# Input norm of a hybrid encoder layer: the row factor moved from the product's operand to its results

## The chip, the cores and the metric

The kernel runs on one core of a Trainium2 chip. The metric is the device time of one execution in microseconds (us), lower is better. The kernel before takes 3166.97 us, the median of three runs (3166.91 to 3171.95).

## The reference

One encoder layer on x of 2048 rows (tokens) by 1024 columns, all in f32:

```python
u = _rms_norm(h, norm_mix_g[l])          # h * rsqrt(mean(h*h) + 1e-6) * g, row by row
proj = u @ w_in[l]                       # 1024 x (1536 + 1024 + 512 + 512 + 16)
hy = _short_conv_centred(proj[..., :HY_COLS], hy_conv_w[l], hy_conv_b[l])      # three taps along the rows
spec = _hyena_filter_spectrum(L, ...)    # a small network with two sines over 2048 positions gives the filters
y_hy = _group_rms_norm(_hyena(hy, spec, hy_skip[l]), hy_norm_g[l], HYENA_GROUPS)   # long convolutions
qk = jax.nn.silu(_short_conv_centred(proj[..., HY_COLS:off], ml_conv_w[l], ml_conv_b[l]))
y_ml = ...                               # bidirectional mLSTM, then a group norm
h = h + concat(y_hy, y_ml) @ w_out[l]
```

Cross attention, a squared-ReLU MLP and a final norm follow. The change touches the first two lines alone: the row factor rsqrt(mean(h*h) + 1e-6) of `u` belongs to a token, the weight g to one of the 1024 columns over which the product sums. So the factor may be multiplied in before the product or after it; g only before.

## The kernel before, in words

**Products.** Each product of f32 operands is made of three: both operands are split into a high half, rounded to the matmul's type by ScalarE (`copy`, shown as CAST), and a low half, the rest, made by VectorE (`split`, L344 and L345). `mm3` (L339 to L342) issues hi by hi, hi by lo and lo by hi into one PSUM bank of 128 by 512.

**The first product, computed transposed.** Columns of `proj` stand on partitions, tokens along the free axis. `sweep` (from L656) takes 256 columns of w_in at a time (`c2`); for each of them two chunks of 512 tokens (`c`) and two halves of 128 columns (`m`); a group is 8 steps of the inner dimension times 3 matmuls, 24 in all. ScalarE copies the full bank to a tile P (L690). When both chunks of a P are there, the short convolution is done in three operations (ScalarE L704, VectorE L706 and L707), and put on `pending`; the next group's end runs `sweep_out`: eight transposes on TensorE (L724), copies, stores to DRAM. Tokens come in two halves of 1024: first `sweep(range(4), 0, True)` on tokens 0 to 1023, then `sweep(range(4), 1, False)` on the others, four 256-column pieces each; the other columns follow later, again by halves.

**The first half's operand.** `x_first` (L489 to L574) prepares tokens 0 to 1023, in chunk 0 (tokens 0 to 511) and chunk 1. x arrives transposed, in loads of two pieces of 128 by 512 each. For chunk 0 ScalarE squares the pieces (L535), VectorE adds them (L537), TensorE sums over partitions (L540), `inv_rms` (L415) makes the factor by Newton steps on a 128 by 4 tile, `diagonal` (L448) and `spread` (L454) turn it into a row on all partitions by a product with ones (L457) and a ScalarE copy (L461). `gained` (L465) multiplies each piece by weight and factor in one VectorE operation; ScalarE makes the high half (L500), VectorE the low half (L502). For chunk 1 the factors come from 2 MB of x in natural layout, whose row sums ScalarE makes as it squares (L422). A function `rest`, run within the first group, writes chunk 1's pieces and starts the stream of weights.

**Work beside it.** `filters` (L234 to L325) runs woven into the sweeps: for four chunks of 512 positions a load of features (L265, issued by SP), a product (L267), a sine (six VectorE operations, L248 to L257, and ScalarE's Sin, L258), a second product (L271) and a second sine; then 32 filter pairs: two products at a time (L177 and L188), VectorE (L317, L318, L322), GpSimd (L323), a transform (`front`, again L177 and L188), ScalarE copies (L301), and a store (L303). The filters and `hy` go through DRAM to the long convolutions (loads `a<-hy`, `a<-fs`; products L845), which are woven with the rest of the sweeps. `row_stats` (L430) makes the row sums of tokens 1024 to 2047, `x_chunk` (L479) their scaled and split pieces, both a step at a time from `pop` in the sweeps. `weights` (L358) loads and splits each next 256 columns in four pieces (L374).

**What sets the order.** The functions issue instructions in program order; a scheduler then places them by priorities along a simulated timeline, held in some places by `keep_in_program_order`. The result is one fixed list per engine, executed in order; each instruction waits for semaphores of those it needs. SP issues most DMAs, also in one fixed order. So a moved operation can shift what stands next to what on every engine.

Of the kernel before, what the change touches and what calls it, by code (L numbers as in the profile page):

```python
# [133 lines left out]
class Prog:  # L134
    def __init__(self, ctx, tc, a):
# [16 lines left out]
        self.banks = []  # L152
        self.pending = []
        self.prepq = None
        self.mid = None
# [333 lines left out]
    def x_first(self):  # L489
        nc, sb = self.nc, self.isb  # L490
        pin = self.tc.keep_in_program_order
        c0, c1 = slice(0, 512), slice(512, 1024)

        def write(xs, cs, rb, between=lambda k: None):
            for k in range(9):
                if k < 8:
                    d = self.gained(xs[k], self.g_mix[:, k:k + 1], rb)
                    if k:
                        pin(d)
                    pin(nc.scalar.copy(self.xh[:, k, cs], xs[k]))  # L500
                if k:
                    nc.vector.tensor_tensor(self.xl[:, k - 1, cs], xs[k - 1], self.xh[:, k - 1, cs].bitcast(F32), ALU.subtract)  # L502
                between(k)

        def pieces(ts):
            return [ts[k // 2][:, k % 2] for k in range(8)]

        x0 = []
# [4 lines left out]
        wsrc = self.items[0][0].rearrange("(k p) c -> p k c", p=128)  # L513
        w0 = [sb.tile([128, 8, 256], F32R, tag=tag, name=tag, bufs=2) for tag in ("wh", "wl")]
        raw = [self.ta().rearrange("p k c -> p (k c)").rearrange("p (k c) -> p k c", k=4) for i in range(2)]
        for i in range(2):
            nc.sync.dma_start(out=raw[i], in_=wsrc[:, 4 * i:4 * i + 4])
        nat = []
        for i in range(4):
            rows = self.a["x"][512 + 128 * i:640 + 128 * i]  # L520
            if i < 2:
                xn = sb.tile([128, D], F32, tag="xn", name="xn", bufs=2)
                nc.sync.dma_start(out=xn, in_=rows)
                nat += [xn[:, 0:512], xn[:, 512:1024]]
            else:
                for h in range(2):
                    xn = self.tb()
                    nc.sync.dma_start(out=xn, in_=rows[:, 512 * h:512 * h + 512])
                    nat.append(xn)
        x1 = pieces([self.x_load(1, j, self.ta()) for j in range(4)])  # L530

        ssum = sb.tile([128, 512], F32, tag="rb", name="ssum", bufs=2)
        for k in range(8):
            sq = sb.tile([128, 512], F32, tag="st", name="sq", bufs=3) if k else ssum
            pin(nc.scalar.activation(sq, x0[k], AF.Square))  # L535
            if k:
                nc.vector.tensor_tensor(ssum, ssum, sq, ALU.add)  # L537
        p = self.mm()
        for t in range(4):
            nc.tensor.matmul(p[:, t:t + 1], ssum[:, 128 * t:128 * t + 128], self.ones[:, 0:1], start=True, stop=True)  # L540
        self.inv_rms(self.rx[:, 0:4], p[:, 0:4])
        dg = self.diagonal(self.rx[:, 0:4])
        ss = sb.tile([128, 2, 4], F32, tag="ss", name="ss", bufs=2)

        def nat_sum(i):
            self.square_sum(nat[i], ss[:, i % 2, i // 2:i // 2 + 1])

        for k in range(0, 8, 2):
            ks = slice(k, k + 2)
            self.split(w0[0][:, ks], w0[1][:, ks], raw[k // 4][:, k % 4:k % 4 + 2])  # L550
        for i in range(4):
            nat_sum(i)
        self.wst = iter((w0,))
        rb = self.spread(dg)
        later = []

        def between(k):
            if k < 4:
                nat_sum(4 + k)
            if k == 4:  # L560
                self.close_sums(self.rx[:, 4:8], ss)
                later.append(self.diagonal(self.rx[:, 4:8]))
        write(x0, c0, rb, between)

        def rest():
            write(x1, c1, self.spread(later[0], True))
            w1 = self.weights(sb, *self.items[1], kc=2, nbufs=3, pin=True)
            self.wst = self.stream(sb, self.items[2:], w1, kc=2, nbufs=3)
        self.mid = rest
        for _ in range(9):  # L570
            yield
        for c in (2, 3):
            yield from self.row_stats(self.rx[:, 4 * c:4 * c + 4], self.a["x"][512 * c:512 * c + 512])
        yield from self.row_stats(self.rm, self.a["mem"])  # L574

    def pop(self, n=1):
        for _ in range(n):
            if self.prepq is not None and next(self.prepq, 0) == 0:
                self.prepq = None

    def prep_x(self, hf):
        self.prepq = chain(self.x_chunk(2 * hf), self.x_chunk(2 * hf + 1))
# [74 lines left out]
    def sweep(self, cols, hf, first, after=None):  # L657
        nc, a, sb = self.nc, self.a, self.isb
        xh, xl, cw, cb, carry = self.xh, self.xl, self.cw, self.cb, self.carry
        for c2 in cols:  # L660
            wh, wl = next(self.wst)
            Ps = []
            if hf == 0:
                off, use, t0, n = 1, 0, 0, 1008 if first else 1040
            elif first:
                off, use, t0, n = 0, 15, 1040, 1008
            else:
                off, use, t0, n = 17, 0, 1008, 1040
            for c in range(2):
                for m in range(2):  # L670
                    yield 5.5
                    cc = carry[:, 2 * c2 + m]
                    ms = slice(128 * m, 128 * m + 128)
                    cs = slice(512 * c, 512 * c + 512)
                    p = self.mm()
                    for k in range(8):
                        self.mm3(p, wh[:, k, ms], wl[:, k, ms], xh[:, k, cs], xl[:, k, cs], k == 0, k == 7)
                        if k == 5 and self.mid is not None:
                            f, self.mid = self.mid, None
                            f()  # L680
                    if c == 0:
                        P = sb.tile([128, 1088], F32, tag="P", name="P", bufs=2)
                        Ps.append(P)
                        edge = 0 if hf == 0 else 1024 if first else 1041
                        nc.vector.memset(P[:, edge:edge + 1], 0.0)  # L685
                        if not first:
                            e0 = 1025 if hf == 0 else 0
                            nc.vector.tensor_copy(P[:, e0:e0 + 17], cc)
                    P = Ps[m]
                    nc.scalar.copy(P[:, off + 512 * c:off + 512 * c + 512], p)  # L690
                    if c == 0:
                        if self.pending:
                            self.pending.pop(0)()
                        self.pop(2)
                        if m == 1 and c2 == cols[-1] and after is not None:
                            after()
                        continue
                    self.pop(3 - 2 * m)
                    if first:
                        nc.vector.tensor_copy(cc, P[:, 1008:1025] if hf == 0 else P[:, 0:17])  # L700
                    ct = 2 * c2 + m
                    cv = sb.tile([128, 1088], F32, tag="cv", name="cv", bufs=2)
                    v = cv[:, 0:n]
                    nc.scalar.activation(v, P[:, use + 1:use + 1 + n], AF.Identity, bias=cb[:, ct:ct + 1],  # L704
                                         scale=cw[:, 1, ct:ct + 1])
                    nc.vector.scalar_tensor_tensor(v, P[:, use:use + n], cw[:, 0, ct:ct + 1], v, ALU.mult, ALU.add)  # L706
                    nc.vector.scalar_tensor_tensor(v, P[:, use + 2:use + 2 + n], cw[:, 2, ct:ct + 1], v, ALU.mult, ALU.add)  # L707
                    if ct >= 12:
                        nc.scalar.activation(v, v, AF.Silu)
                        if ct >= 16:  # L710
                            nc.vector.tensor_scalar(v, v, 128.0 ** -0.5, None, ALU.mult)
                    self.pending.append(lambda ct=ct, cv=cv, t0=t0, n=n: self.sweep_out(ct, cv, t0, n))

    def sweep_out(self, ct, cv, t0, n):
        nc, sb = self.nc, self.isb
        v = cv[:, 0:n]
# [1224 lines left out]
def program(p):  # L1941
    with ExitStack() as ms:
        with ExitStack() as es:
# [79 lines left out]
```

## Time and profile before

| | |
|---|---|
| median of three runs | 3166.97 us |
| the profiled execution | 3178.03 us, span 3176.3 us |
| mean granted TensorE clock | 0.982 |
| HBM | 191 GB/s over the span |
| costliest group on VectorE | L345, low halves of weights, 289.5 us busy |

How to read it: the span runs from the first to the last instruction of one profiled execution. Busy time of an engine is what its instructions took; matmuls are pipelined, so the busy times of neighbouring ones overlap, and what one costs is the distance to the start of the next. In the lists of groups a row has line, engine, operation, result and operands, count, busy time, mean of one, and the idle time before them with what ended it. In the timeline a row begins with start and busy time in us, and ends with the idle time before it and what released it, in brackets. The granted clock is a share of TensorE's full speed. PEld is TensorE loading weights.

### The profile page before, as it was taken

Reading aid. Unit: us, or ns where it says so; the run is one execution under the profiler, and the core shown is the slowest. Engines: PE = TensorE matmul, PEld = TensorE weight load, DVE = VectorE, ACT = ScalarE, POOL = GpSimd, SP = SyncE. Lnnn points to the kernel's source line nnn. Section 1 sums busy time; section 2 is a strip of 40 time slices with the busy share of each in tenths; the row PEclk is TensorE's granted clock in tenths of the full one; section 3 lists DMA queues with packets and bytes.
Section 4 is the critical chain, followed back from the end, with each engine's and each line's share of the span. In section 5 each row is a group of like instructions: output and inputs, shape, how many; then the busy total and the mean of one; then the engine's idle time right before and its main releaser. Section 6 shows DMA issues by size and latency. Waiting matters only on the chain.

```text
span 3176.3 us, 43590 instructions
## 1 busy us (share of the span) xinstructions
PE 3039.3 (96%) x14473; PEld 2393.8 (75%) x14473; DVE 2048.0 (64%) x3563; ACT 1503.0 (47%) x2873; POOL 1157.8 (36%) x802
## 2 busy tenths in 40 slices
PE   6999999999999976999999999999999999999998
PEld 4655566776668766788888888888888878888876
DVE  7775466434865676878766566657655686565695
ACT  5543366523675343445454455556555443333335
POOL 0122012100112334324231426776555483434483
PEclk9999999999999998999999999999999999999999
DMA  5554767686576988547374747656644474444434
GB/s 190 191 196 162 255 194 205 180 253 212 165 226 191 309 256 263 172 144 231 114 272 144 274 131 246 203 194 221 216 155 146 163 243 147 144 129 152 123 93 169
DMA packets 447673, 609.48 MB, mean 192 GB/s; under 512 B 39118, under 2 KB 249166, under 8 KB 446424
## 3 DMA queue, kind: packets, MB, share of 16 engines
q1 hardware_dynamic: 409268, 548.18, 54.7%
q10 hardware_dynamic: 38180, 58.51, 5.5%
q8 instruction: 115, 1.88, 0.2%
q14 instruction: 110, 0.90, 0.1%
HBM read 404.15 MB, written 202.41 MB: 191 GB/s over the span
## 4 chain that ended last, share of the span: by engine, by line
PE 79%; DMA 8%; DVE 7%; issue 3%; ACT 2%; POOL 1%; SPq 0%; ACTq 0%; DVEq 0%; POOLq 0%
PE mm L340 17%; PE mm L342 17%; PE mm L341 17%; PE hy L342 5%; PE hy L340 5%; PE hy L341 5%; PE hy L177 3%; PE hy L876 2%; PE mm L845 2%; PE hy L918 1%; DMA xt<-in_x_t_dram 1%; DVE wl L345 1%; PE hy L1213 1%; PE hy L1082 1%; PE hy L1215 1%
## 5 line engine op out<-in xcount | busy, mean ns | idle before, releaser
L345 DVE TENSOR_TENSOR wl<-wn,wh 128x512 fp32r<-128x512 f32 (+1 forms) x364 | 289.5, 830 | 128.9 <-ACT wh L345 128.7
L1558 DVE TENSOR_TENSOR bl<-wr,bh 128x512 fp32r<-128x512 f32 x213 | 239.1, 1129 | 130.8 <-ACT bh L1557 130.6
L1557 ACT CAST ah<-w 128x512 fp32r<-128x512 f32 x284 | 176.7, 623 | 303.3 <-PE hy L341 156.1
L345 ACT CAST wh<-wn 128x512 fp32r<-128x512 f32 (+1 forms) x364 | 208.1, 619 | 218.7 <-PE mm L342 51.2
L923 POOL TENSOR_TENSOR b<-b,a 128x512 f32<-128x512 f32 x64 | 87.2, 1363 | 586.8 <-ACT b L921 463.2
L340 PE MATMUL mm<-xh,wh 128*128 128x512 f32 x640 | 271.6, 425 | 3.7 <-ACT xh L500 2.3
L341 PE MATMUL mm<-xl,wh 128*128 128x512 f32 x640 | 257.9, 404 | 2.4 <-DVE xl L345 1.8
L342 PE MATMUL mm<-xh,wl 128*128 128x512 f32 x640 | 259.2, 405 | 0.0
L1557 ACT CAST bh<-wr 128x512 fp32r<-128x512 f32 x232 | 143.7, 621 | 233.3 <-PE mm L342 181.1
L1558 DVE TENSOR_TENSOR al<-w,ah 128x512 fp32r<-128x512 f32 x236 | 214.4, 909 | 54.3 <-ACT ah L1557 52.9
L342 PE MATMUL mm<-bh,al 128*128 128x512 f32 x576 | 225.3, 394 | 7.3 <-DVE al L1558 4.7
L340 PE MATMUL mm<-bh,ah 128*128 128x512 f32 x576 | 226.9, 394 | 1.0 <-DVE acc L1715 0.9
L341 PE MATMUL mm<-bl,ah 128*128 128x512 f32 x576 | 226.1, 393 | 0.0
L340 PE MATMUL mm<-act,wh 128*128 128x512 f32 x512 | 198.4, 393 | 2.6 <-ACT wh L345 1.3
L341 PE MATMUL mm<-act,wh 128*128 128x512 f32 x512 | 200.4, 392 | 0.2 <-DVE act L345 0.2
L342 PE MATMUL mm<-act,wl 128*128 128x512 f32 x512 | 199.0, 391 | 0.0
L340 PE MATMUL hy<-bh,ah 128*128 128x512 f32 x448 | 175.2, 391 | 0.0
L341 PE MATMUL hy<-bl,ah 128*128 128x512 f32 x448 | 174.6, 390 | 0.0
L342 PE MATMUL hy<-bh,al 128*128 128x512 f32 x448 | 174.4, 390 | 0.0
L340 PEld LDWEIGHTS mm<-xh,wh 128*128 128x128 f32 x640 | 122.0, 191 | 65.7 <-issue 29.2
L341 PEld LDWEIGHTS mm<-xl,wh 128*128 128x128 f32 x640 | 121.6, 190 | 53.0 <-issue 24.4
L323 POOL TENSOR_TENSOR b<-b 128x512 f32<-128x512 f32 x32 | 59.1, 1848 | 275.8 <-DVE P L685 127.8
(378 smaller groups left out, 8487.2 us busy)
## 6 DMA issues: line engine op xcount, KB each, us to landing
wr<-hc SPq DMA_DIRECT2D x224, 256.0 KB
w<-in_ff_w_dram SPq DMA_DIRECT2D x172, 256.0 KB
hc<-wn SPq DMA_DIRECT2D x128, 256.0 KB
wn<-in_w_in_dram SPq DMA_DIRECT2D x100, 256.0 KB
hc<-q SPq DMA_DIRECT2D x96, 256.0 KB
fs<-a SPq DMA_DIRECT2D x32, 512.0 KB
a<-fs SPq DMA_DIRECT2D x64, 256.0 KB
a<-zs SPq DMA_DIRECT2D x64, 256.0 KB
```

What stands on the lines that cost most here:

```text
L177: b = self.nc.tensor.matmul(*products[-1], start=True, stop=True)
L323: nc.gpsimd.tensor_tensor(e[1], f, b, ALU.subtract)
L340: mm(ps, lh, rh, start=start, stop=False)
L341: mm(ps, lh, rl, start=False, stop=False)
L342: mm(ps, ll, rh, start=False, stop=stop)
L345: both = (self.nc.scalar.copy(hi, src), self.nc.vector.tensor_tensor(lo, src, hi.bitcast(F32), ALU.subtract))
L845: nc.tensor.matmul(pp, dm[:, m], t[:, m], start=True, stop=True)
L876: nc.tensor.matmul(pg, em[:, m], y, start=True, stop=True)
L918: nc.tensor.matmul(pp, dm[:, m], t[:, m], start=True, stop=True)
L923: nc.gpsimd.tensor_tensor(xt, xt, hi[:, m], ALU.mult)
L1557: self.nc.scalar.copy(hi, src)
L1558: eng.tensor_tensor(lo, src, hi.bitcast(F32), ALU.subtract)
```

## The change

The pieces of the first 1024 tokens are multiplied by g alone: ScalarE makes the high half from x as a copy scaled by g, VectorE the low half from x in one operation. Nothing of chunk 0's operand needs the row factor any more. The loads of x and of the first weights alternate; the 2 MB in natural layout are not loaded. Squares of chunk 0 come after its split; a function `second` run in group 0 makes chunk 1's operand, starts the weights and squares chunk 1; `scales`, run in group 1, makes column sums, factors and rows for both chunks into `rowb[0]` and `rowb[1]`. What was done as a bank is left is put into a closure `leave`, kept on a list `lag` for up to three groups (fewer towards the eighth), and in the first sweep over the first half VectorE multiplies the bank by `rowb[c]` as it writes P, in place of ScalarE's copy. Later sweeps copy as before. A pool `x_o` for the sums and rows is closed between the two sweeps by `opened`. Which pending store is run, and when `pop` is called, moves slightly.

```diff
+        for j in range(4):                      # x_first, loads
             x0.append(self.x_load(0, j, ...))
+            if j % 2 == 0:
+                nc.sync.dma_start(out=raw[j // 2], in_=wsrc[:, 2 * j:2 * j + 4])
...
+        def operand(xs, c, k):
+            to = (slice(None), k, slice(512 * c, 512 * c + 512))
+            g = self.g_mix[:, k:k + 1]
+            pin(nc.scalar.activation(self.xh[to], xs[k], AF.Copy, scale=g))
+            nc.vector.scalar_tensor_tensor(self.xl[to], xs[k], g, self.xh[to].bitcast(F32), ALU.mult, ALU.subtract)
...
+        def columns(c):
+            p = self.hy()
+            for t in range(4):
+                nc.tensor.matmul(p[:, t:t + 1], ssum[c][:, 128 * t:128 * t + 128], self.ones[:, 0:1], start=True, stop=True)
+            rx = self.rx[:, 4 * c:4 * c + 4]
+            self.inv_rms(rx, p[:, 0:4])
+            self.dg = self.diagonal(rx)
+
+        def rows(c):
+            p = self.hy()
+            nc.tensor.matmul(p, self.ones, self.dg, start=True, stop=True)
+            nc.scalar.copy(self.rowb[c], p)
...
+        def second():
+            for k in range(8):
+                operand(x1, 1, k)
+            w1 = self.weights(sb, *self.items[1], kc=2, nbufs=3, pin=True)
+            self.wst = self.stream(sb, self.items[2:], w1, kc=2, nbufs=3)
+            squares(x1, 1)
+
+        def scales():
+            for c in range(2):
+                columns(c)
+                rows(c)
+
+        self.hooks = {(0, 5): second, (1, 5): scales}
...
                     for k in range(8):                      # sweep
+                        if (self.made, k) in self.hooks:
+                            self.hooks.pop((self.made, k))()
                         self.mm3(p, wh[:, k, ms], wl[:, k, ms], xh[:, k, cs], xl[:, k, cs], k == 0, k == 7)
-                    P = Ps[m]
-                    nc.scalar.copy(P[:, off + 512 * c:off + 512 * c + 512], p)
...
+                    def leave(c=c, m=m, c2=c2, p=p, cc=cc, Ps=Ps):
...
+                        to = P[:, off + 512 * c:off + 512 * c + 512]
+                        if hf == 0 and first:
+                            nc.vector.tensor_tensor(to, p, self.rowb[c], ALU.mult)
+                        else:
+                            nc.scalar.copy(to, p)
...
+                    if self.pending and (c == 0 or len(self.pending) > 1):
+                        self.pending.pop(0)()
+                    self.lag.append(leave)
+                    while len(self.lag) > max(0, min(3, 8 - self.made)):
+                        self.lag.pop(0)()
+                    self.made += 1
...
-            s = chain(p.sweep(range(4), 0, True, lambda: p.prep_x(1)), p.sweep(range(4), 1, False))
+            s = chain(p.sweep(range(4), 0, True, lambda: p.prep_x(1)), p.opened(), p.sweep(range(4), 1, False))
```

More of the change, by code (lines that the diff above doesn't have):

```diff
@@ L491, in x_first @@
         pin = self.tc.keep_in_program_order
[L492 to L503, printed above, removed]
+        self.xes = ExitStack()
+        xo = self.xes.enter_context(self.tc.tile_pool(name="x_o", bufs=1))
+        ssum = [xo.tile([128, 512], F32, name=f"ssum{c}") for c in range(2)]
+        self.rowb = [xo.tile([128, 512], F32, name=f"rowb{c}") for c in range(2)]
         def pieces(ts):
             return [ts[k // 2][:, k % 2] for k in range(8)]
+        wsrc = self.items[0][0].rearrange("(k p) c -> p k c", p=128)
+        w0 = [sb.tile([128, 8, 256], F32R, tag=tag, name=tag, bufs=2) for tag in ("wh", "wl")]
+        raw = [self.ta().rearrange("p k c -> p (k c)").rearrange("p (k c) -> p k c", k=4) for i in range(2)]
         x0 = []
@@ new lines, in squares @@
+        def squares(xs, c):
+            for k in range(8):
+                sq = sb.tile([128, 512], F32, tag="st", name="sq", bufs=3) if k else ssum[c]
+                pin(nc.scalar.activation(sq, xs[k], AF.Square))
+                if k:
+                    nc.vector.tensor_tensor(ssum[c], ssum[c], sq, ALU.add)
+        def columns(c):
[5 more added lines that the diff above has]
+            self.dg = self.diagonal(rx)
@@ L579, in pop, with opened @@
                 self.prepq = None
+    def opened(self):
+        self.xes.close()
+        return
+        yield
     def prep_x(self, hf):
@@ L689, in sweep @@
-                    P = Ps[m]
[L690 to L700, printed above, removed]
```

106 lines of the change are left out of this document (35 added, 71 removed).

## The prediction

> **What bounds the kernel now.** I read the page first, then the windows of the first 400 us, then the timeline at the places where a window shows TensorE idle, and beside these the order of instructions of both programs, engine by engine (it holds no times).
>
> ```profile
> span 3176.3 us, 43590 instructions
> PE 3039.3 (96%) x14473; PEld 2393.8 (75%) x14473; DVE 2048.0 (64%) x3563; ACT 1503.0 (47%) x2873; POOL 1157.8 (36%) x802
> PE 79%; DMA 8%; DVE 7%; issue 3%; ACT 2%; POOL 1%; SPq 0%; ACTq 0%; DVEq 0%; POOLq 0%
> ```
>
> TensorE is busy 96% of the span and carries 79% of the chain that ended last. The change removes hardly any of its work, so it can only win TensorE's idle or half-clock time, or add to it. The columns of the windows are: stretch and length, then busy time and instructions of PE, PEld, DVE, ACT and POOL, the granted clock, the DMA share and GB/s.
>
> ```profile
> 0.00:25.00 25.00, 4.80 (x12) 2.71 (x12) 13.60 (x39) 12.89 (x26) 0.70 (x6) 1.00 0.95 345
> 25.00:62.00 37.00, 32.35 (x113) 22.73 (x114) 33.52 (x72) 20.47 (x37) 0.00 (x0) 0.91 0.24 73
> 62.00:92.00 30.00, 30.00 (x138) 24.03 (x138) 23.88 (x55) 22.67 (x50) 0.00 (x0) 1.00 0.69 205
> 92.00:118.00 26.00, 24.36 (x103) 19.03 (x101) 16.31 (x29) 12.70 (x23) 0.00 (x0) 0.93 0.63 221
> 118.00:200.00 82.00, 80.19 (x358) 45.93 (x358) 68.08 (x116) 34.69 (x53) 19.24 (x10) 1.00 0.55 180
> 200.00:300.00 100.00, 99.55 (x477) 57.81 (x477) 57.92 (x89) 36.81 (x64) 28.98 (x16) 1.00 0.56 189
> 300.00:370.00 70.00, 69.65 (x327) 43.52 (x324) 35.33 (x53) 27.02 (x45) 10.90 (x6) 1.00 0.60 194
> 370.00:400.00 30.00, 23.35 (x83) 11.39 (x82) 9.09 (x13) 7.97 (x13) 0.00 (x0) 0.89 0.84 306
> ```
>
> Three places can give time: the first 24 us (TensorE waits for x and the row factor), 25 to 62 us (VectorE, busy 33.5 of 37, paces it), and 370 to 400 us (6.7 us idle and some at the lower clock, DMA share 0.84).
>
> **The change, part by part.**
>
> *The start.* Before, ScalarE squares the pieces as they land, and the weights' halves come after all of x:
>
> ```profile
> 5.87 0.63 ACT L535 ACTIVATE ssum<-xt 128x512 f32<-128x512 f32 x1 [2.26 <-DMA xt<-in_x_t_dram]
> 8.81 1.15 ACT L535 ACTIVATE sq<-xt 128x512 f32<-128x512 f32 x2 [1.79 <-DMA xt<-in_x_t_dram]
> 13.01 1.14 ACT L345 CAST wh<-a 128x512 fp32r<-128x512 f32 x2 [0.30 <-DMA a<-in_w_in_dram]
> 24.14 0.79 PE L340 MATMUL mm<-xh,wh 128*128 128x512 f32 x1 [2.11 <-ACT xh L500]
> 62.36 0.57 ACT L690 COPY P<-mm 128x512 f32<-128x512 f32 x1
> ```
>
> The loads of 512 KB land at 5.87, 8.81 and then some 1.4 us apart, the fifth at 13.01. In the changed order the first weight half takes the second place, so it lands at 8.8; one cast (0.57, half of the 1.14 of two) lets the first product start at about 9.4 instead of 24.14. From there a piece costs ScalarE one copy (0.57) and VectorE one operation with two inputs and a scalar. The prices on VectorE, and the pitch of a matmul at both clocks:
>
> ```profile
> 26.31 0.63 PE L341 MATMUL mm<-xl,wh 128*128 128x512 f32 x1
> 26.74 0.63 PE L342 MATMUL mm<-xh,wl 128*128 128x512 f32 x1
> 43.02 0.40 PE L341 MATMUL mm<-xl,wh 128*128 128x512 f32 x1
> 43.26 0.39 PE L342 MATMUL mm<-xh,wl 128*128 128x512 f32 x1
> 44.27 0.75 DVE L465 SCALAR_TENSOR_TENSOR a<-a,par,rb 128x512 f32<-128x512 f32 x1
> 44.93 0.69 DVE L502 TENSOR_TENSOR xl<-a,xh 128x512 fp32r<-128x512 f32 x1
> ...
> 120.30 0.68 DVE L317 TENSOR_TENSOR b<-hy,a 128x512 f32<-128x512 f32 x1
> ```
>
> The new operation is of L465's kind: 0.66 from its start to the next one's. Before, a piece took that and a subtraction (some 0.60); the change saves 16 subtractions, 9.6 us of VectorE, and 16 ScalarE copies become copies with a scale (taken as equal; bounds 0.57 and the 0.63 of L535). A matmul's pitch is 0.43 cold and some 0.23 warm. Walked through the changed order with these prices, the 96 matmuls of the first 256 columns end at about 34 (before 62.36).
>
> *The factor, later.* The two factors are now made behind the second product: column sums, Newton steps, a diagonal, a product with ones and a ScalarE copy stand behind the splits, the squares and the next weights' casts on VectorE and ScalarE. I get the diagonal at 34.0, the row at 37.4, the first multiplied bank at 38.0; all banks are full by then, so TensorE stands 3 us, and 0.6 for the second factor. The multiplication moves 16 bank copies from ScalarE (0.57 each, L690) to VectorE, 9.6 us at 0.60; that pays back what the subtractions saved. After eight groups of 24 matmuls the changed kernel stands near 63.5, the present one at 85.7 (62.36, four groups of 24 x 0.228 and 1.4 of the filter network's products); 6 us of that is side work not yet done (transposes), so **some 16 us ahead**. 2 MB of natural rows need no longer come before the second chunk of x, which hides under the first products.
>
> The Trainium skill, "Perfetto Trace Analysis", section "Optimizing Scalar/DVE Operations", gives a VectorE operation an access overhead of some 60 ns on SBUF and some 125 ns on PSUM; by it the 16 multiplications would cost 16 x 0.065 = 1 us more, an estimate, and the sum +8. L317 already reads a bank (0.68 against L502's 0.69), so the trace gives no such addition and my sum has none.
>
> *The filter network.* Here the order turns against the change. The features' second chunk is loaded by SP behind weight loads that wait for buffers:
>
> ```profile
> 53.90 9.90 SPq L374 DMA_DIRECT2D wn<-in_w_in_dram  x6
> 56.71 0.62 ACT L345 CAST wh<-wn 128x512 fp32r<-128x512 f32 x1 [3.15 <-DMA wn<-in_w_in_dram]
> 72.53 1.02 PE L267 MATMUL hy<-b,fw 66*128 66x512 f32 x2
> 73.39 1.04 PE L724 MATMUL mm<-ident,cv 128*126 128x128 f32 x8
> 74.19 0.48 PE L340 MATMUL mm<-xh,wh 128*128 128x512 f32 x1
> 109.03 0.81 DVE L248 TENSOR_SCALAR b<-hy,par 128x512 f32<-128x512 f32 x1 [4.41 <-PE hy L271]
> 112.34 0.43 DVE L257 TENSOR_SCALAR b<-b 128x512 f32<-128x512 f32 x1
> 112.80 1.15 ACT L258 ACTIVATE hid<-b 128x512 f32<-128x512 f32 x1 [1.03 <-DVE b L257]
> 118.04 0.69 PE L177 MATMUL hy<-fw,hid 64*128 64x512 f32 x1
> ```
>
> A load lands some 2.8 us after issue (53.90 to 56.71). L267 costs 0.86 (72.53 to 73.39), eight transposes 0.80. One sine takes VectorE 3.74 (109.03 to the end of L257, 112.77), then ScalarE 0.6 (half of 1.15, the first of two). Before, sweep products stand between the network's L267 and L271 products, so these waits are mostly hidden: 92 to 118 us has TensorE idle 1.6 us and a clock of 0.93. In the changed order seven such products, L267 and L271 in turn and then the first L177, stand **directly one after another** on TensorE with no sweep product between them. Each L271 waits for a sine, and from the second on for two, since VectorE has the previous chunk's other sine ahead. With the second chunk of features landing near 73: L267 at 73.9, the three L271 at 81.6, 90.7 and 99.8, the first L177 at 105.7. Of these 32 us the network's own products and what stands beside them cover 4 to 5; **27 us are stall**.
>
> Now compare equal work. The first L177 comes at 118.04 before, with 301 sweep products done (counted in the order); it comes at 105.7 after, with 216. The 85 missing ones cost 85 x 0.228 = 19.4. 118.04 - 105.7 = 12.3 earlier, less 19.4: **7 us behind**. The 16 us of the start and some 4 of waits are spent.
>
> The Trainium skill, "TensorE: Matmul & The Clock Gate", section "Part 1: The HAM clock gate", says that an idle window of some 3.4 us drops TensorE to half clock and that it takes about as long under load to come back; by it every return from the waits above starts cold, and counted twice (after the network and after the next stall) the sum would be +9. The trace agrees in kind (0.43 at 26.31, after the long first wait). My sum counts one cold return, since the next stall follows within a few us of the first.
>
> *The first filter pairs.* ScalarE's row sums of the third chunk cost, a piece:
>
> ```profile
> 67.31 0.65 ACT L422 ACTIVATE junk<-xn 128x512 f32<-128x512 f32 x1
> ```
>
> In the changed order VectorE's first pair work stands behind these row sums (0.65 a piece and the gap to the next), themselves behind the network's last sine; the product after the pair waits for it until about 113.7, a stall of 6 us, and 1.7 for the cold clock. **About 15 us behind** near 130 us.
>
> *The passage to the long convolutions.* In the present order seven L177 pairs of that stage stand with no sweep products between, as its loads come slowly:
>
> ```profile
> 384.63 0.66 PE L177 MATMUL hy<-a,f 64*128 64x512 f32 x1 [1.81 <-DMA a<-hy]
> ...
> 388.98 3.75 PE mm L845 x4
> 409.70 1.72 PE mm L845 x4
> ...
> PE hy L918 <- DMA a<-zs: 1.8, 1, 1.8
> ```
>
> Idle 6.7 (30.00 - 23.35), 2.0 from products at the cold clock (L845: 3.75 for four against 1.72), 2.6 of idle between 118 and 370, and 1.8 of another wait (L918): 13 us of losses. In the changed order the filters end earlier (120 sweep products earlier), so sweep products stand 24 between one such pair and the next: these 13 go. For the changed kernel's own losses in that stretch (VectorE has some 40 us of work on the second half of x beside 38 of TensorE) I take 5, bounds 3 and 13. Both reach the first product of the next stage with the same 984 sweep products done, 15 - 13 + 5 = **7 us behind**.
>
> *After it.* TensorE's order is the same from there to some 1030 us, and differs little up to 1300 us; I take nothing, bounds -5 and +5.
>
> Sum: -16 (start, made of 14.7 earlier first product and a shorter first group, net of later waits) turned into +7 by the network, +8 by the first pairs, -13 + 5 by the passage: +7 us. The profiled execution took 3178.0 us (its span of 3176.3 and 1.7 around it), 11 above the median of 3166.97; I add the sum to each: 3185 for an execution like the profiled, **3174 us** for the median.
>
> **The rivals.**
>
> 1. *Slower still, the passage gives nothing.* The stretch from 375 to 395 us ran at 306 GB/s and a DMA share of 0.84; if the convolutions' loads, not the order, set its end, the changed kernel starves there too: +15 to +20, 3184. Against it: 24 sweep products between pairs are 5.5 us of cover each.
> 2. *Faster: the network's chain is shorter than I make it.* Place: 64 to 106 us. If the second features are in by 64, and VectorE has one sine rather than two between two L271, a link costs 3.74 + 0.6 + 0.86 = 5.2 instead of 9.1. The stall then falls from 27 to some 7 to 11, worth 16 to 20: 7 - 18 = -11, 3156. It decides from a link of about 6.5 us (three links, 2.6 less each, and 5 from an earlier start, bring the sum to -6). Against it: the order on VectorE and SP, which I followed row by row.
> 3. *Repaid exactly.* The parts are large (-16, +23, +8, -8) and their sum small: with 2 to 4 us of error it is within 6.3 us of nothing: 3168.
> 4. *It doesn't do what it says.* If the second 256 columns wait for the factor as long as the present kernel waits at its start, the early start is worth nothing: the row would have to come at about 54 instead of 37. Then +7 + 14, 3188. The order puts only splits and squares ahead of it, so I give it little.
>
> **How the numbers follow.** Forecast 0.37 (3170 to 3180), rival 1 0.18, rival 2 0.17, rival 3 0.23, rival 4 0.05. About 0.2% (6.3 us) is what a measurement of this kernel can tell from no change. My forecast of +7 lies just beyond it; half of its cases within (0.13) and rival 3's go to the same, leaving slower 0.47, same 0.36, faster 0.17. As both signs hold a share, the forecast's own range is 3170 to 3180; the range for all, from halfway to rival 2 to rival 4's end, is 3158 to 3189.
>
> **What would show it.** The first L340 at 9 to 10 us; a wait of some 3 us on the multiplied bank before the second 256 columns; L267 and L271 one by one between 70 and 106 us with idle TensorE and a low clock in 75 to 110; the first L177 at 103 to 108; sweep products between the convolutions' pairs near 380 us and a clock of 1.00 there. I am wrong if the network's stall is under 15 us or over 35, if the passage still idles by over 8 us, or if the stretch after 420 us differs by more than 5.

## The result

The changed kernel takes 3187.53 us, the median of six runs (3177.36 to 3188.66), against 3169.46 us for the kernel before beside them (3165.97 to 3175.22). The ratio is 1.0047 (95% interval 1.0034 to 1.0061): **slower by some 15 us** (the two medians by themselves lie 18 apart), where the prediction had 7 us. The 3187.5 lie above the forecast's own range of 3170 to 3180 and within the range for all, 3158 to 3189. Its profiled execution took 3182.6 us, span 3180.9. The page of the changed kernel, span, busy times and chain:

```profile
span 3180.9 us, 43576 instructions
PE 3036.8 (95%) x14481; PEld 2392.0 (75%) x14481; DVE 2061.5 (65%) x3569; ACT 1494.6 (47%) x2849; POOL 1146.2 (36%) x802
PE 78%; DVE 8%; DMA 6%; issue 3%; ACT 3%; POOL 1%; SPq 0%; ACTq 0%; DVEq 0%; POOLq 0%
```

TensorE has the same work as before (3036.8 busy against 3039.3). What changed is where it stands idle. The windows of the changed kernel, cut as in the prediction (PE, PEld, DVE, ACT and POOL busy, granted clock, DMA share, GB/s):

```profile
0.00:25.00 25.00, 15.03 (x61) 12.33 (x61) 16.09 (x28) 17.79 (x29) 0.70 (x6) 1.00 0.91 321
25.00:62.00 37.00, 33.64 (x135) 25.90 (x135) 24.93 (x64) 12.24 (x21) 0.00 (x0) 0.91 0.20 58
62.00:92.00 30.00, 18.29 (x71) 12.16 (x69) 23.87 (x43) 9.23 (x11) 0.00 (x0) 0.78 0.16 49
92.00:118.00 26.00, 9.64 (x14) 2.86 (x14) 16.05 (x32) 9.54 (x24) 1.05 (x1) 0.53 0.35 121
118.00:200.00 82.00, 77.97 (x360) 45.15 (x362) 59.60 (x117) 33.91 (x66) 20.75 (x12) 0.96 0.65 217
200.00:300.00 100.00, 98.06 (x456) 56.78 (x453) 73.47 (x111) 40.64 (x66) 25.95 (x15) 1.00 0.59 205
300.00:370.00 70.00, 69.48 (x320) 43.22 (x318) 34.43 (x52) 26.82 (x45) 7.97 (x5) 1.00 0.64 204
370.00:400.00 30.00, 30.00 (x136) 21.58 (x135) 13.06 (x20) 10.92 (x19) 0.00 (x0) 1.00 0.88 299
```

The first row gains (61 matmuls against 12) and the last one too (30.00 of 30 busy against 23.35). Between them, from 62 to 118 us, TensorE is busy 28 of 56 us, at a granted clock of 0.53 in the second window; before it was busy 54 of these 56. The timeline of TensorE in the changed kernel, the start first:

```profile
9.97 0.79 PE L340 MATMUL mm<-xh,wh 128*128 128x512 f32 x1 [9.97 <-ACT wh L345]
38.57 0.79 PE L340 MATMUL mm<-xh,wh 128*128 128x512 f32 x1 [2.81 <-DVE P L687]
55.81 0.50 PE L340 MATMUL mm<-xh,wh 128*128 128x512 f32 x1 [0.54 <-DVE P L687]
...
77.05 1.10 PE L267 MATMUL hy<-b,fw 66*128 66x512 f32 x2 [0.30 <-DMA b<-in_c_feat_dram]
85.07 2.07 PE L271 MATMUL hy<-b,fw 128*128 128x512 f32 x2 [6.93 <-ACT b L258]
86.93 1.91 PE L267 MATMUL hy<-b,fw 66*128 66x512 f32 x2
95.17 2.07 PE L271 MATMUL hy<-b,fw 128*128 128x512 f32 x2 [6.33 <-ACT b L258]
97.04 1.91 PE L267 MATMUL hy<-b,fw 66*128 66x512 f32 x2
105.34 2.07 PE L271 MATMUL hy<-b,fw 128*128 128x512 f32 x2 [6.38 <-ACT b L258]
112.25 1.22 PE L177 MATMUL hy<-fw,hid 64*128 64x512 f32 x1 [4.84 <-ACT hid L258]
```

Six products of the filter network and the first filter pair's stand with nothing between them; the three L271 wait over 6 us each for a sine. The distance from one L271 to the next, a link of this chain, can be followed: L271 at 85.07, L267 at 86.93, then 6.33 us of idle to the next L271. The windows of this stretch (columns as above; the granted clock follows POOL):

```profile
87.00:97.00 10.00, 3.67 (x5) 1.11 (x4) 6.86 (x12) 1.71 (x2) 0.00 (x0) 0.50 0.34 118
97.00:113.00 16.00, 4.78 (x7) 1.34 (x7) 10.33 (x18) 6.14 (x14) 0.00 (x0) 0.50 0.21 66
```

For the comparisons I part each span in three. **Front**: up to the start of the last product of the long convolutions' transform (L876, `hy<-b,em`; L878 or so in the others). **Middle**: from there to the first `mm<-wh,act` product, the stretch with the busiest DMAs. **Rest**: to the end. In all kernels but e5 and e7 the same TensorE products, but for some small ones of the factor, stand in each part, so these times are taken at equal work. With the kernel before and the changed one profiled a second time (`e11` and `e12`, below):

| profiled execution | span | front | middle | rest |
|---|---|---|---|---|
| before | 3176.3 | 1023.2 | 318.5 | 1834.6 |
| before, again | 3169.2 | 1019.8 | 317.8 | 1831.6 |
| changed | 3180.9 | 1035.1 | 312.5 | 1833.3 |
| changed, again | 3183.8 | 1035.2 | 312.6 | 1836.0 |

The change costs 12 to 15 us in the front. It gains 5 to 6 us in the middle, in code that it doesn't touch: there some 110 VectorE rows, 84 of TensorE and 40 to 46 each of ScalarE and SP stand in another order in the two. Where such parts are compared below, each kernel but these two has one profile, and the two of the kernel before differ by 3.4 us in the front.

### The profile page after: what moved, and what is told of

Read it like the earlier page. It is cut to its first block, busy times and chain, and to the rows that moved or that the text cites. A ratio compares the mean times of both kernels' runs of the same rounds, so it can differ in the third digit from the quotient of the medians.

```text
span 3180.9 us, 43576 instructions
## 1 busy us (share of the span) xinstructions
PE 3036.8 (95%) x14481; PEld 2392.0 (75%) x14481; DVE 2061.5 (65%) x3569; ACT 1494.6 (47%) x2849; POOL 1146.2 (36%) x802
## 4 chain that ended last, share of the span: by engine, by line
PE 78%; DVE 8%; DMA 6%; issue 3%; ACT 3%; POOL 1%; SPq 0%; ACTq 0%; DVEq 0%; POOLq 0%
PE mm L340 17%; PE mm L342 17%; PE mm L341 17%; PE hy L340 5%; PE hy L342 5%; PE hy L341 5%; PE hy L177 3%; PE hy L878 2%; PE mm L847 1%; PE hy L920 1%; DVE bl L1560 1%; DVE wl L345 1%; DMA xt<-in_x_t_dram 1%; PE hy L1215 1%; DMA wn<-in_xa_wv_dram 1%
## 5 line engine op out<-in xcount | busy, mean ns | idle before, releaser
L340 PE MATMUL mm<-wh,xh 128*128 128x256 f32 (+1 forms) x512 | 152.9, 300 | 5.4 <-ACT st L203 3.4
```

The lines of the kernel that those rows point to most:

```text
L340: mm(ps, lh, rh, start=start, stop=False)
```

## The experiments

Three theories. **A**: the order of the instructions makes the loss: network products stand bunched on TensorE, and each waits for sines on VectorE. **B**: SP makes it, since the features are loaded behind weight loads that wait. **C**: VectorE's added work (bank multiplications) makes it, wherever it stands. D and E are rivals of single runs and told there. "With n sweep products done" means below: at the start of the next one, counted in the trace; a sweep product is one matmul of `sweep` (24 to a group). Each time is a median beside runs of the kernel before on the same chip (3171.8, 3171.2 and 3172.0 in the three groups).

### e1: features ahead

```diff
         x1 = pieces([self.x_load(1, j, self.ta()) for j in range(4)])
+        self.feats = self.fsb.tile([128, 2048], F32, name="feats")
+        pin(nc.sync.dma_start(out=self.feats[0:66], in_=self.a["c_feat"]))
...
-                nc.sync.dma_start(out=feat[0:66], in_=a["c_feat"][:, cs])
-                nc.tensor.matmul(p1, w1, feat[0:66], start=True, stop=True)
+                nc.tensor.matmul(p1, w1, self.feats[0:66, cs], start=True, stop=True)
```

> The changed kernel with the filter network's four loads of features made one, ahead of the weights' loads. The order of TensorE's products is the same as in the changed kernel. Theory A (the order on TensorE makes the stall: network products one after another with two sines between, and VectorE's bank multiplications behind the sines): the features' wait was only 0.3 us, so the links stay near 10.1 us, first L177 at 110 to 113, time as the changed kernel within 4 us (3183 to 3191). Theory B (SP's late feature loads make the stall): first L177 at 100 or earlier, 3172 to 3178.

3194.5 us, ratio 1.0069 (1.0049 to 1.0089). SP's queue in the changed kernel, then in this one (start, how long the queue took with them, count):

```profile
40.34 33.52 SPq L374 DMA_DIRECT2D wn<-in_w_in_dram  x5
73.92 16.77 SPq L265 DMA_DIRECT2D b<-in_c_feat_dram  x3
```

```profile
11.06 0.47 SPq L510 DMA_DIRECT2D feats<-in_c_feat_dram  x1
```

And what TensorE waited for in this one from 25 to 125 us (total, times, longest):

```profile
PE hy L269 <- ACT b L258: 17.3, 3, 6.1
PE hy L177 <- ACT hid L258: 4.9, 1, 4.9
```

The load that stood at 73.92 is issued 63 us earlier, and the waits for sines are as before (19.6 in three and 4.8 in the changed kernel). The front falls by 2 us only (1033.0), and the first L177 comes at 110.04, as A has it. B alone is out. The total is 3.5 us above A's range: the middle takes 324.7 us, 12 more than in the changed kernel.

### e2 and e3: the bank leaves without VectorE

```diff
-                            nc.vector.tensor_tensor(to, p, self.rowb[c], ALU.mult)
+                            nc.scalar.copy(to, p)
+                            nc.vector.tensor_tensor(to, to, self.rowb[c], ALU.mult)      # e2
+                            nc.gpsimd.tensor_tensor(to, to, self.rowb[c], ALU.mult)      # e3, in its place
```

> The changed kernel, but ScalarE copies the bank to P and VectorE multiplies P by the factor in SBUF, so that a bank is free without VectorE. VectorE has as many operations as in the changed kernel. Theory A: the network's products stand spread between 177 and 457 sweep products in the order, the stall between 77 and 123 us is gone (TensorE idle there under 5 us), and by 200 us the kernel is 20 us or more ahead of the changed one at equal work; but the filters end later (936 sweep products), so the passage to the long convolutions starves again and gives 13 to 20 us back: 3155 to 3172. Theory C (VectorE's added work is what costs): no better than the changed kernel, 3184 to 3190.

> As the kernel with ScalarE's copy, but GpSimd multiplies P by the factor in SBUF; VectorE loses 16 operations (9.6 us). Theory A: as that kernel within 5 us, 3153 to 3170, since VectorE is not the bound there. Theory C: 8 to 12 us faster than that kernel.

3202.2 us (1.0096, 1.0083 to 1.0108) and 3201.1 us (1.0085, 1.007 to 1.0099). Both are the slowest of all, and yet the stall of the network is gone: their waits between 25 and 125 us come to 6.3 and 7.4 us, none of more than 0.4 us for a sine. With 768 sweep products done they are 29.6 and 32.8 us ahead of the kernel before. It is lost behind that, e2 from 350 to 420 us (windows, then waits from 300 to 420):

```profile
350.00:380.00 30.00, 15.89 (x74) 3.79 (x72) 13.06 (x18) 8.14 (x14) 8.51 (x5) 0.77 0.40 150
380.00:420.00 40.00, 21.59 (x61) 8.88 (x62) 8.99 (x13) 7.30 (x13) 0.00 (x0) 0.71 0.93 299
```

```profile
PE hy L177 <- DMA a<-hy: 16.5, 4, 11.8
PE mm L848 <- issue: 7.7, 1, 7.7
```

The sweeps have run ahead of the filters: the last filter product stands behind 936 sweep products, not 713, and the order puts none between the long convolutions' loads. So with banks that are left without VectorE the network no longer stands bunched and its stall is gone, as A has it, but taking it away by itself makes things worse. Both totals are some 30 us above A's ranges: I had priced the passage at 13 to 20 us, and from 768 to 1056 sweep products done it took e2 60 us more than the kernel before (-29.6 to +30.8). By its total e2 fits C ("no better"), but e3, with 9.6 us less on VectorE, gains 1 us on it where C asked for 8 to 12.

### e4, e6 and e8: fewer shared banks

Column sums and row of the factor (`columns`, `rows`) take their banks from the same four (`hy`) as the network, and banks of one tag are given out in program order. In the changed order the network's first product (L267 at 54.25) stands right behind the factor's last one (L535 at 53.39), at 144 sweep products.

```diff
         def columns(c):
             p = self.hy()
+            self.bank = p
...
         def rows(c):
-            p = self.hy()
+            p = self.bank
```

e6 is this alone, e4 this with e1's features, e8 is e4 with the squares added by GpSimd.

> The changed kernel with features ahead and with column sums and row of a chunk in one bank, so that the factor takes two of the four banks that it shares with the filter network instead of four. The order then starts the network at 121 sweep products instead of 144, and leaves two links instead of three at 216. Theory A: the stall at 216 is shorter by one link, 8 to 11 us, 3175 to 3180. Theory B: as with the features ahead alone.

> The changed kernel with a chunk's column sums and row in one bank, features loaded as in the changed kernel. It parts the two edits of the run with one bank and early features. Theory A: the bank alone does it, 3172 to 3180, first L177 at 100 to 105. Theory B (features): 3184 to 3192.

> The kernel with one bank and early features, and GpSimd adds the squares (14 operations, 8.4 us less on VectorE). The order at 216 sweep products stays as bunched as there. Theory A: the stall at 216 is set by two sines a link and does not care for VectorE's load before it, within 4 us of that kernel, 3170 to 3178. Theory C: 6 to 9 us faster than that kernel, 3165 to 3168.

e4 3174.4 us (1.001, 0.9999 to 1.0021), e6 3191.2 us (1.0063, 1.005 to 1.0076), e8 3195.2 us (1.0071, 1.0057 to 1.0085). By the fronts: 1035.1 in the changed kernel, 1033.0 with features alone, 1028.4 with one bank alone, **1021.9 with both**. So B has a part: once the banks let the network start, late features hold it. In e6, from 25 to 125 us, TensorE waits for them:

```profile
PE hy L267 <- DMA b<-in_c_feat_dram: 2.0, 1, 2.0
```

The two together are worth 13 us in the front, their sum is 9; that they are worth more together isn't shown, for the difference is near the 3.4 us between two profiles of one kernel. At the first L177, with 216 sweep products done in all four, features alone bring 2 us (110.04 against 112.25), one bank 8 (103.91) and both 11 (100.93). The network in e4:

```profile
74.25 1.02 PE L269 MATMUL hy<-b,fw 128*128 128x512 f32 x2
75.11 1.02 PE L265 MATMUL hy<-feats,fw 66*128 66x512 f32 x2
84.60 2.07 PE L269 MATMUL hy<-b,fw 128*128 128x512 f32 x2 [8.02 <-ACT b L258]
86.47 1.91 PE L265 MATMUL hy<-feats,fw 66*128 66x512 f32 x2
93.94 2.08 PE L269 MATMUL hy<-b,fw 128*128 128x512 f32 x2 [5.56 <-ACT b L258]
100.93 1.22 PE L177 MATMUL hy<-fw,hid 64*128 64x512 f32 x1 [4.91 <-ACT hid L258]
```

One link less stands behind the sweep products than above, and the first L177 comes at 100.93 instead of 112.25, with as many sweep products done (216). e6's total lies in B's range (3184 to 3192), but its first L177 comes at 103.91, as A has it; the total has another reason, its middle: 325.3 against e4's 313.1. e8 missed both ranges, and doesn't tell what the added squares cost VectorE: GpSimd takes 11 us for seven of them in a row, so the factor comes later (the first multiplied bank ends TensorE's wait at 44.67, in e4 at 38.26) and the front is 1033.7; its middle of 328.7 adds 16 us more than e4's.

### e5 and e10: the passage by itself, in the kernel before

```diff
-            weave(s, p.filters(), 140, 80, True)
+            weave(s, p.filters(), 160, 80, True)      # e5
```

e10 is the kernel before with e1's edit (there the features ahead do move the network).

> The kernel before, with one number of the weave changed (140 to 160), so that four more groups of sweep products come behind the start of the long convolutions in program order. The order of the first 888 sweep products stays; the long convolutions' seven bunched pairs now have sweep products between. It tests the passage's term alone: theory A prices the passage at 13 us lost in the kernel before, so this gains 8 to 13 us, 3157 to 3164, with TensorE idle under 1 us between 370 and 400 us. Rival D (the DMA sets the end of that stage, whatever the order): 3168 to 3172.

> The kernel before with the features loaded in one DMA ahead of the weights. Its order puts the network at 15, 80, 120 and 175 sweep products and the first filter pair at 226 instead of 301, and the filters' end at 737 instead of 816, so that the long convolutions' pairs have sweep products between them (812 to 936) as in the changed kernel, with the weave as it is. Theory A: 8 to 12 us of the passage's 13 are gained and not given back later, since no group of sweep products is moved ahead of the long convolutions' start; its order from 1030 to 1345 us is the changed kernel's, some 4 us slower: 3160 to 3168. Rival E (the passage's gain is always given back): 3168 to 3176.

e5: 3188.8 us (1.0053, 1.0041 to 1.0066). e10: **3152.8 us (0.9944, 0.9931 to 0.9956)**, the fastest kernel of the study. Windows of the kernel before (profiled again), then e5, then e10:

```profile
380.00:420.00 40.00, 33.42 (x128) 22.19 (x126) 18.58 (x30) 17.69 (x30) 3.69 (x3) 0.91 0.72 230
1050.00:1100.00 50.00, 46.60 (x332) 39.99 (x330) 33.65 (x80) 17.27 (x34) 17.11 (x12) 0.97 1.01 310
1100.00:1200.00 100.00, 77.45 (x468) 64.80 (x469) 70.82 (x165) 38.25 (x75) 38.61 (x30) 0.90 0.87 267
1200.00:1300.00 100.00, 72.66 (x434) 64.26 (x432) 75.55 (x232) 44.23 (x155) 43.12 (x33) 0.85 0.76 238
```

```profile
380.00:420.00 40.00, 40.00 (x175) 28.73 (x174) 20.88 (x32) 20.24 (x31) 0.00 (x0) 1.00 0.76 244
1050.00:1100.00 50.00, 36.07 (x216) 28.77 (x215) 29.78 (x60) 14.11 (x27) 14.11 (x9) 0.86 0.91 265
1100.00:1200.00 100.00, 76.14 (x431) 61.26 (x430) 73.38 (x173) 40.08 (x79) 36.82 (x28) 0.88 0.87 262
1200.00:1300.00 100.00, 65.16 (x365) 59.06 (x364) 65.98 (x210) 32.44 (x120) 39.20 (x33) 0.74 0.72 230
```

```profile
380.00:420.00 40.00, 38.65 (x156) 26.92 (x155) 24.04 (x35) 23.16 (x38) 3.49 (x3) 1.00 0.57 155
1050.00:1100.00 50.00, 44.68 (x298) 36.46 (x297) 37.40 (x86) 17.58 (x33) 17.99 (x13) 0.93 1.01 307
1100.00:1200.00 100.00, 80.58 (x470) 67.21 (x468) 64.70 (x156) 41.02 (x80) 30.37 (x27) 0.88 0.86 269
1200.00:1300.00 100.00, 80.47 (x459) 72.12 (x459) 82.85 (x247) 45.84 (x158) 45.02 (x35) 0.83 0.73 237
```

In e5 the passage is full (40.00 of 40), so the order and not the DMA sets it: rival D is out, at a DMA share of 0.76. But the expected 3157 to 3164 are missed by 25 us. The sweep products, and the products of later stages that are woven in behind them, now come early: with 1824 sweep products done e5 is 31 us ahead, and at its last L876 (1037.8, some 15 us late) it has done 252 products more than the kernel before, 25 us of TensorE. So it is still some 10 us ahead in work there, and the loss lies behind: its middle takes as long (317.7) for 252 products less. From 1050 to 1300 us TensorE is busy 177.4 instead of 196.7. (The windows are cut at the same times, not at the same work.) The gain is given back and more: the woven products are the filler of the starved stages, and there is one supply of them. In e10 the filters end 79 sweep products earlier (737 instead of 816), and each part holds the same products as in the kernel before; front 1010.6, 9 to 13 us less, and middle 313.5, 4 to 5 less. Rival E holds for e5 and not for e10, which came out 7 us below theory A's range.

### e7: everything spread

e4 with e3's multiplication and the weave at 180.

> Early features, one bank for each chunk's factor, ScalarE's copy of the bank with GpSimd's multiplication in SBUF, and the weave at 180. In the order the network stands spread from 141 to 345 sweep products, and ten of the convolutions' pairs have sweep products between, seven still stand together. Theory A: no stall of the network (TensorE idle under 5 us between 40 and 130 us), and less of a passage than the run with GpSimd's multiplication alone, which lost some 45 us there: 3150 to 3172. Theory C (VectorE's added work costs): VectorE has 9.6 us less, 3178 at best.

3192.0 us (1.0065, 1.0052 to 1.0078). No wait over 3 us from 25 to 350 us, 39 us ahead with 960 sweep products done, and then as e5: busy 180.4 from 1050 to 1300 us, the last L876 at 1036.4 with the same 252 products more done. Theory A's 3150 to 3172 are missed. The total fits C's "3178 at best", but the loss lies far behind the last multiplied bank (131 us), so it doesn't speak for C.

### e9: a shorter lag

```diff
-                    while len(self.lag) > max(0, min(3, 8 - self.made)):
+                    while len(self.lag) > max(0, min(1, 8 - self.made)):
```

in e4.

> The kernel with one bank for a chunk's factor and early features, and with the lag of the bank's multiplication cut from three groups to one, so that VectorE's multiplications stand earlier in program order, ahead of the network's sines. In the order the network stands at 120, 135, 184 and 259 sweep products and the first filter pair at 306 (216 with a lag of three), the filters end at 809. Theory A (the order makes the stall, here by the multiplications that stand behind the sines): no wait of more than 3 us for a sine after 216 sweep products, and at 1030 us 8 to 18 us ahead of the kernel before. The stretch from 1030 to 1345 us has the order of the three runs that lost 13 to 15 us there beside the kernel before, so 3163 to 3178 in all. Theory C (VectorE's load): not ahead at 1030 us.

3176.2 us (1.0004, 0.9994 to 1.0014), front 1019.3, as the kernel before (1019.8 and 1023.2): **the expectation of 8 to 18 us ahead failed**, though the total lies within the expected 3163 to 3178. That is luck: its middle took 321.8 us, 3 to 4 more than in the kernel before, where 13 to 15 were expected. Its waits from 25 to 125 us, then the longest of them and what VectorE does behind it:

```profile
PE mm L727 <- DVE cv L701: 7.7, 1, 7.7
PE hy L269 <- ACT b L258: 4.4, 1, 4.4
PE mm L338 <- DVE P L688: 2.8, 1, 2.8
```

```profile
66.65 1.94 PE L727 MATMUL mm<-ident,cv 128*126 128x128 f32 x8 [7.73 <-DVE cv L701]
68.63 0.69 DVE L205 COPY st<-mm 126x512 f32<-126x512 f32 x1
74.71 0.81 DVE L248 TENSOR_SCALAR b<-hy,par 128x512 f32<-128x512 f32 x1 [5.39 <-PE hy L269]
```

The bunch at 216 sweep products is gone, but TensorE then waits 7.7 us for VectorE's short convolution, which now stands behind sines and multiplications. That is the outcome which C gave, and during that wait VectorE works without a gap. But right behind it VectorE stands idle for 5.39 us until TensorE's L269, and from 25 to 92 us it is busy only 50 of 67: what binds is that its queue and TensorE's chain wait for each other in turn. With the network spread, VectorE is late with something else, and the 14 us of the earlier start are spent either way.

### e11 and e12: both kernels again

> The kernel before once more, for its profile: where the profiled execution (3178) lies above the median (3170). Expected: the first 1030 us the same within 2 us, the difference between 1030 and 1345 us, where the DMAs are busiest.

> The changed kernel once more, for its profile: its first profiled execution (3182.6) lies 5 below the median (3187.5). Expected: 12 us behind the kernel before at 1030 us as in the first, within 2 us, and the difference from the first profile between 1030 and 1345 us.

3170.9 and 3185.5 us. The changed kernel is 12.0 behind the first profile of the kernel before at the end of the front, as expected, and 15.4 behind the second. That the differences between profiles of one kernel lie in the middle was wrong: there they agree within 0.7 us. They are 3.4 in the front and 3.0 in the rest for the kernel before.

## Why the prediction was right in its sign and too small

- *The start*: right. First product at 9.97 (9.4 forecast), the wait for the multiplied bank 2.81 (3), for the second factor 0.54 (0.6). After eight groups the changed kernel is 18.4 us ahead of the kernel before (67.7 against 86.1 with 192 sweep products done); I had 63.5 against 85.7, gross 22. Of the 4 us between, some 3 are the clock behind the wait (0.63 from 38 to 47 us): the first 14 products after it take 6.1 us, 3.2 at 0.228 each.
- *The filter network*: the right mechanism, too small. **This is the term that failed**: "7 us behind" at the first filter product measured 13.6 (112.25 with 216 sweep products against 118.04 with 301: 19.4 - 5.8). The first L177 came 6.6 us later than forecast (112.25 against 105.7). The chain started 3.2 us later (L267 at 77.05, not 73.9: TensorE had waited 1.33 us for a multiplied bank just before, and the features, whose load SP issued at 73.92 only, landed 0.30 us after it was ready for them); the links took 10.1 us, not 9.1, and the other two stretches of the chain 1.3 us more. A pair of network products between two waits took some 3.8 us (L271 at 85.07, L267 at 86.93 and 1.9 more), where I put 0.86 for each.
- I had put one cold return into the sum. The Trainium skill, "TensorE: Matmul & The Clock Gate", "Part 1: The HAM clock gate", puts TensorE at half clock after an idle window of some 3.4 us, so that every return from such a wait would start cold. The trace agrees: all four waits of the chain are over 4.8 us, the clock from 87 to 113 us is 0.50, and the L271 behind the waits take 2.07 where the L267 at 77.05 took 1.10. I weighed that rule and counted it once, though a sum over the whole chain was at hand.
- *The first filter pairs and the stretch to the filters' end*: 13.6 behind became 22.0 (last filter product at 330.8 with 713 sweep products against 332.3 with 816): 8.4 lost. The forecast had 8, 5 for the changed kernel's own losses, less the 2.6 of idle in the kernel before that it counts to the passage: 10.4. (The filters end 103 sweep products earlier, not 120.)
- *The passage*: 22.0 became 13.5 with 1152 sweep products done, 8.5 gained, where the rest of the -13 was 10.4. From the first L177 to here the forecast has 0 in all, and -0.1 came. The window from 370 to 400 us is full, as forecast. Rival 1 gave nearly the measured time (3184), but not by its mechanism: the passage did give. (Its 306 GB/s and 0.84 are those of 370 to 400 us; from 375 to 395 it was 341 and 0.91.)
- *After it*: "I take nothing, bounds -5 and +5". By the first profiles 13.5 behind became 4.6, of which 6 in the middle: that is beyond the bounds, and one of the signs of being wrong that the prediction named. By the second profiles 14.8 became 14.6, 5 gained in the middle and 4 lost in the rest. So what is left of the gap to the medians (15 to 18 us against 4.6 between the first two profiles) is a matter of single executions: the first profile of the kernel before lies 8 to 11 us above its medians and that of the changed kernel 5 below its own.
- *Rivals 2, 3 and 4* didn't occur: a link was longer, not shorter; the interval of the ratio, 1.0034 to 1.0061, leaves out no change; and the second columns started at 38.57. (In the chances, 0.13 is a third of 0.37 and not the half that the text calls it.)

The cause, as far as the runs show it: bank sharing and the features' place in SP's queue, together, make 13 of the front's 12 to 15 us (e4: 1021.9 instead of 1035.1, the kernel before 1019.8 and 1023.2). That is the loss against the kernel before; the 14 us by which the first product comes earlier are still spent in e4, on the links that are left: 17.8 us ahead of the kernel before with 192 sweep products done, it is 2.3 behind at the first L177 (19.4 - 17.1). Why a spread network (e9) still only draws level with the kernel before is not settled: the waits name VectorE's queue, and no run takes them away without moving the filters. No edit that kept the changed kernel's start came out faster than the kernel before.

What stays open is the middle. Its length seems to go with the order of instructions there: 312.5 to 313.5 us in the changed kernel, e4 and e10, which differ there in some ten to forty rows of an engine, 318 in the kernel before, 321.8 in e9, 325 to 329 in e1, e6 and e8, which share another order. But e2, whose order there is as near to the changed kernel's (at most 26 rows of an engine differ), took 318.5. In both pairs of profiles most of the changed kernel's gain falls near 1235 to 1280 us, in shorter waits of the products `hy<-va,rw` and `hy<-ve,kn` (the longest, 6.30 and 5.84 us in the kernel before, is 4.43 and 3.12 in the changed one). Which of the moved rows does it wasn't tried.

## What to carry to other kernels

An edit at the start of a kernel whose order is made by a scheduler moves everything behind it: compare the two orders on each engine, count what stands between dependent products on the bottleneck engine, and price each bunch, at the half clock where the waits are long. Ask too from which pool the moved operations take their buffers: a chain that shares a rotating pool with another one holds it up, though no data pass between them. And filler work is one supply here: a stall that is closed by pulling filler forward comes back where the filler is missing, so a stall is better closed by making its producer earlier (e10: 0.9944) than by spending cover on it (e5: 1.0053).

## What the runs showed of the hardware

GpSimd's additions of 128x512 in f32 took 1.27 to 1.78 us each (11.03 for seven in a row, e8), against VectorE's 0.69 in the changed kernel: as a chain they put the first multiplied bank 6 us later (44.67 against 38.26 in e4). One of the network's f32 products was busy 1.02 us at the full clock (e4, 74.25) and 1.91 to 2.07 behind the waits; with waits of 5 to 7 us between, the granted clock was 0.50 from 87 to 113 us of the changed kernel. Two profiles of the kernel before differ by 7 us in span (3169.2 and 3176.3), 3.4 in the front and 3.0 in the rest, while a middle stretch that is the same code in another order moved by 16 us (312.5 to 328.7).
